# A hybrid decoder trunk on one core: the parts of the attention are moved to later items of the program

## The chip, the cores and the metric

The kernel runs on one NeuronCore of a Trainium2 chip. The metric is the device time of one execution in microseconds, the median of the runs shown. PE is the matmul engine, PEld its weight loads, ACT the scalar engine, DVE the vector engine, POOL the general one, SP the engine whose queue issues most DMAs. PSUM is the memory that PE writes, SBUF the working memory.

## The reference

Two layers on 512 tokens of width 1024, all in float32. Cut to what matters:

```python
h = rmsnorm(x, g_mix[l])
dq, dk, dv, c_q, c_kv_kr, xq, gate_logits = jnp.split(h @ w_in[l], split_idx, axis=-1)
y_diff = diff_attention(dq, dk, dv, ...) @ w_diff_o[l]       # 8 heads, 2 causal softmaxes each: (p0 - lam * p1) v
y_mla = latent_attention(c_q, c_kv_kr, ...) @ w_mla_o[l]     # 8 causal heads, q and k of 96
y_mem = memory_cross_attention(xq, mem_n, ...) @ w_cross_o[l]  # 4 heads into 256 memory tokens
gates = jax.nn.sigmoid((gate_logits + b_gate[l]).reshape(B, S, N_BRANCHES, D))
merged = gates[:, :, 0] * y_diff + gates[:, :, 1] * y_mla + gates[:, :, 2] * y_mem
x = x + merged @ w_out[l]
x = x + jnp.square(jax.nn.relu(rmsnorm(x, g_mlp[l]) @ w_mlp1[l])) @ w_mlp2[l]
```

Queries, keys and several latents are normalised by their root mean square, and queries and keys are rotated by position.

## The kernel before

Weights stream from HBM in units of 128 x 1024 numbers. Each unit is split into a high part `whi` (written by ACT, L101) and a low part `wlo` (DVE, L102), and a product is three matmuls of the parts (`mm3`, L109 to L111). Three raw units and four split ones are held.

A layer is a list of entries, each a function that issues its instructions and the weight units that it needs. `phases` lists the attention entries ("items" here): four head pairs of latent attention (`mla_att`), four cross heads, eight heads of differential attention (`diff_att`), each head with four items, one for each block of 128 queries (cross: two). `PLAN` lists the projections (entries of matmuls with weights) that belong to each phase, and `merge` puts them between the items, about one or two behind each. The projections are: K0, K1, Q0, Q1 (`kvb_item`, `qb_item`) for the latent attention, `mem_chunk`, `xq_chunk`, `head_chunk` (queries and keys of one differential head), `v_chunk`, `gate_item`, and `y4_item`, the output products of the cross and latent attention. Behind the last phase stand `y8_item` (output product of the differential attention), `out_item`, and the MLP.

An item of differential attention does all its parts in one entry: `scores` (matmuls L622, mask L634, maximum L636, exponential L639, the two maps joined at L644), then `pv_tok`: one PE transpose for each block of 128 keys (L650), a copy to SBUF (tile PT, L95), and the value products (L654) into the bank `pso`. After the fourth item, `o_copy` and `o_finish` normalise the head's output and transpose it (L681). Latent and cross attention use L625 for scores, `turned` (transposes L666, copies to the two PT tiles of a split) and `mm3` into `pso`. Projections that need rows turned into columns transpose at the end of their entry: `heads_T` (L482) for keys and queries of the latent attention, L360 and L395 for memory keys and cross queries, L597 for differential heads, the last behind a chain of DVE work that ends at L593.

Pools with few buffers matter: PSUM has two banks `psacc` (projections), three `pss` (scores), two `pstp` (transposes) and one `pso` (values). In SBUF there are three probability tiles `P`, four `PT` and five `scr`.

The order on each engine is made at build time. The library's planner takes the program's instructions with their dependences, runs a timing model of the engines, and at each moment gives an engine the earliest one in the program that the model holds ready; each engine then executes its list strictly in that order, waiting where the real time differs.

Of the kernel before, what the change touches and what calls it, by code (L numbers as in the profile page):

```python
# [59 lines left out]
def tile_trunk(ctx: ExitStack, tc: tile.TileContext, x_t, mem_t, mem_n, pos, ifr, gcol, grow, w_ck, w_cq, w_kvb, w_qb,  # L60
# [36 lines left out]
    def scale_to(o, i, col):  # L97
        A.activation(out=o, in_=i, func=AF.Copy, scale=col)
# [182 lines left out]
    def layer(l):  # L281
        col = lambda c, n=P: gc[:n, l, c:c + 1]
        s = {}

        def build_rope():
# [55 lines left out]
        def mem_chunk(c):  # L341
            def done(tp, q):
                if c < 2:
# [12 lines left out]
                    V.tensor_tensor(out=yv, in0=yv, in1=f[:, :4].unsqueeze(2).broadcast_to([P, 4, 128]), op=ALU.mult)  # L356
                    tp_ = ps("tp")
                    for h in range(2):
                        for t in range(2):
                            T.transpose(tp_[:, h * 256 + t * P:h * 256 + (t + 1) * P], in_=yv[:, t * 2 + h, :], identity=ident)  # L360
                    o = tl("B")
                    scale_to(o, tp_, col(C_CK))
                    s["mk"].append(o)
                else:
# [10 lines left out]
        def xq_chunk(c):  # L375
            def done(tp, q):
# [14 lines left out]
                V.tensor_tensor(out=yv, in0=yv, in1=f[:, :4].unsqueeze(2).broadcast_to([P, 4, 128]), op=ALU.mult)  # L391
                tp_ = ps("tp")
                for h in range(2):
                    for t in range(2):
                        T.transpose(tp_[:, h * 256 + t * P:h * 256 + (t + 1) * P], in_=yv[:, t * 2 + h, :], identity=ident)  # L395
                for h in range(2):
                    scale_to(s["xq", c][h][:, tp * 256:(tp + 1) * 256], tp_[:, h * 256:(h + 1) * 256], col(C_CQ))
            return chunk256(w_xq[l, c], x_h, 4, done)
# [88 lines left out]
        def kvb_item(hf):  # L487
            def fn(w):
# [31 lines left out]
                s["kT", hf], s["v", hf] = [], vv  # L520
                heads_T(kc, s["kT", hf], col(C_MK, 96))
            return Entry(fn, [w_kvb[l, hf]])

        def qb_item(hf):
            def fn(w):
# [26 lines left out]
                s["qT", hf] = []  # L552
                heads_T(qt, s["qT", hf], col(C_MQ, 96))
            return Entry(fn, [w_qb[l, hf][:, 0:2, :], w_qb[l, hf][:, 2:3, :]])
# [10 lines left out]
        def head_chunk(h):  # L565
            def done(tp, q):
# [26 lines left out]
                V.tensor_tensor(out=yg, in0=yg, in1=f.unsqueeze(2).broadcast_to([P, 8, 64]), op=ALU.mult)  # L593
                tp_ = ps("tp")
                for c in range(2):
                    for t in range(2):
                        T.transpose(tp_[:, c * 256 + t * P:c * 256 + (t + 1) * P], in_=y[:, t * 256 + c * P:t * 256 + (c + 1) * P], identity=ident)  # L597
                sl = slice(tp * 256, (tp + 1) * 256)
                for m in range(2):
                    own, oth = slice(m * 64, (m + 1) * 64), slice((1 - m) * 64, (2 - m) * 64)  # L600
                    qs, ks = tp_[own, 0:256], tp_[own, 256:512]
                    copy_to(qh[m][own, sl], qs)
                    copy_to(kk[m][own, sl], ks)
                    copy_to(qh[m][oth, sl], qs)
                    V.tensor_tensor(out=ql[m][own, sl], in0=qs, in1=qh[m][own, sl], op=ALU.subtract)
                    V.tensor_tensor(out=kk[m][oth, sl], in0=ks, in1=kk[m][own, sl], op=ALU.subtract)
            return chunk256(w_d[l, h], x_h, 4, done)
# [38 lines left out]

        def pv_tok(pt, nb, o, vs):
            tp_ = ps("tp")
            for j in range(nb):
                T.transpose(tp_[:, j * P:(j + 1) * P], in_=pt[:, 0, j * P:(j + 1) * P], identity=ident)  # L650
            w = tl("PT")
            copy_to(w[:, :nb * P], tp_[:, :nb * P])
            for j in range(nb):
                T.matmul(o, lhsT=w[:, j * P:(j + 1) * P], rhs=vs(j), start=j == 0, stop=j == nb - 1)  # L654

# [20 lines left out]
        def o_finish(o, f, ng, gain, key):  # L676
            ov = o.rearrange("p (g d) -> p g d", g=ng)
            V.tensor_tensor(out=ov, in0=ov, in1=f.unsqueeze(2).broadcast_to([P, ng, 512 // ng]), op=ALU.mult)
            tp_ = ps("tp")
            for t in range(NT):  # L680
                T.transpose(tp_[:, t * P:(t + 1) * P], in_=o[:, t * P:(t + 1) * P], identity=ident)  # L681
            hi, lo = tl("O", F32R), tl("O", F32R)
            split_scaled(hi, lo, tp_, gain)
            s.setdefault(key, []).append((hi, lo))

        def o_copy():
            c = tl("scr")
            A.activation(out=c, in_=s["co"], func=AF.Copy)
            return c

        def cross_att(h):
            c, hh = h // 2, h % 2

            def unit(qp):
                def fn(w):
                    if qp == 0:
                        s["co"] = ps("o")
# [4 lines left out]
                    w = turned([pt[:, m, j * P:(j + 1) * P] for j in range(2) for m in range(2)])  # L702
                    for j in range(2):
                        mm3(s["co"][:, qp * 256:(qp + 1) * 256], tuple(z[:, j * 256 + hh * P:j * 256 + (hh + 1) * P] for z in s["mv"][c]), tuple(z[:, j * 256:(j + 1) * 256] for z in w), j == 0, j == 1)
                    if qp == 1:
                        o_split("oc")
                return Entry(fn)
            return [unit(0), unit(1)]

        def mla_att(hp):  # L710
            hf, h0 = hp // 2, (hp % 2) * 2

            def unit(qi):
                def fn(w):
# [8 lines left out]
                    pair = (s["pe"], pt)  # L723
                    o = ps("o")
                    ov = o.rearrange("p (m q t) -> p m q t", m=2, q=2)
                    for j in range(qi + 1):
                        g = 1 if j == qi else 0
                        w = turned([x[:, m, j * P:(j + 1) * P] for m in range(2) for x in pair[g:]])
                        f = (j % 2) * 256 + h0 * 64
                        mm3(ov[:, :, 1, :] if g else o, tuple(z[:, f:f + P] for z in s["v", hf][j // 2]),  # L730
                            tuple(z[:, :256] if g else z for z in w), j == 0, j == qi, skip_group_check=True)
                    if qi == 1:
                        s["oT"] = tl("O", F32R), tl("O", F32R)
                    hi, lo = s["oT"]
                    sl = slice((qi - 1) * P, (qi + 1) * P)
                    for m in range(2):
                        r = slice(m * 64, (m + 1) * 64)
                        split_into(hi[r, sl], lo[r, sl], o[r, m * 256:(m + 1) * 256])
                    if qi == NT - 1:
                        s.setdefault("om", []).append((hi, lo))  # L740
                return Entry(fn)
            return [unit(q) for q in range(NT)]

        def diff_att(h):
            p, hh = h // 2, h % 2

            def unit(qi):
                def fn(w):
                    if qi == 0:
                        s["co"], s["cs"] = ps("o"), small("osum", 8, 3)  # L750
                    N = P * (qi + 1)
                    o, cs = s["co"], s["cs"].rearrange("p (m q) -> p m q", m=2)
                    qh, ql, kk = s["dh", h]
# [4 lines left out]
                    pt = scores(N, qk, True, [cs[:, m, qi:qi + 1] for m in range(2)], True)  # L758
                    pv_tok(pt, qi + 1, o[:, qi * P:(qi + 1) * P], vf)
                    if qi == NT - 1:  # L760
                        oc = o_copy()
                        z = tl("scr")
# [7 lines left out]
                        rsq(f[:, :4], e[:, :4], 4)  # L770
                        o_finish(oc, f[:, :4], 4, dgain[:, l:l + 1], "od")
                return Entry(fn)
            return [unit(q) for q in range(NT)]
# [251 lines left out]
```

## Time and profile before

| | us |
|---|---|
| median of 3 runs (lowest to highest) | 2017.84 (2017.49 to 2018.43) |
| the profiled execution's own time | 2019.04 |
| its span, first to last instruction | 2017.2 |
| PE busy | 1976.3 (98%) |
| DVE busy | 1187.2 (59%) |
| ACT busy | 961.9 (48%) |

Times in the rows are from the start of the span. Layer 0 ends near 1017 us, and layer 1 repeats it. Matmuls are pipelined, so the busy time of one is longer than the distance between two.

### The profile page before, as it was taken

What the parts mean: (1) busy time and instruction counts of PE and PEld (TensorE: products, weight loads), DVE (VectorE), ACT (ScalarE), POOL (GpSimd) and SP (SyncE); (2) the same over time, 40 slices, a digit from 0 to 9 for tenths busy, and PEclk for the clock granted to TensorE, in tenths of its full rate; (3) what the DMA queues carried; (4) which work ended last, traced back from release to release, by engine and by line L of the source; (5) the groups of instructions that cost most, each with busy time, mean ns of one, the idle gap of its engine ahead of it and who ended that gap; (6) DMA issues with size and microseconds to landing.
All of it is one profiled execution on the core that took longest, in us unless ns stands there. A gap on an engine that the chain in (4) does not pass through costs nothing.

```text
span 2017.2 us, 27896 instructions
## 1 busy us (share of the span) xinstructions
PE 1976.3 (98%) x10880; PEld 1711.2 (85%) x10880; DVE 1187.2 (59%) x2235; ACT 961.9 (48%) x1855; POOL 155.7 (8%) x153
## 2 busy tenths in 40 slices
PE   8999999999999999999999999999999999999999
PEld 7778989888888888888888899988888888888887
DVE  7756677687745443434447667678777554434442
ACT  5766765555533432323347667556555333323321
POOL 0300101111100000000002001011111000000000
PEclk9989999999999999999999999999999999999999
DMA  5233222222224333333332321221222333333332
GB/s 170 73 107 105 64 64 69 69 71 66 74 76 149 92 102 94 94 100 100 114 109 65 124 86 53 72 76 63 63 74 74 115 115 94 95 95 101 97 94 73
DMA packets 54676, 181.06 MB, mean 90 GB/s; under 512 B 6417, under 2 KB 7441, under 8 KB 54545
## 3 DMA queue, kind: packets, MB, share of 16 engines
q1 hardware_dynamic: 51840, 175.66, 28.1%
q10 hardware_dynamic: 2704, 3.62, 0.6%
q8 instruction: 86, 1.41, 0.3%
q14 instruction: 46, 0.37, 0.1%
HBM read 175.06 MB, written 4.19 MB: 89 GB/s over the span
## 4 chain that ended last, share of the span: by engine, by line
PE 91%; DVE 5%; ACT 2%; issue 1%; DMA 1%; POOL 0%; ACTq 0%; DVEq 0%; POOLq 0%
PE psacc L109 19%; PE psacc L110 19%; PE psacc L111 19%; PE pss L111 7%; PE pss L109 7%; PE pss L110 7%; PE pss L625 2%; PE pso L654 2%; PE pss L622 2%; PE pstp L666 1%; PE pstp L650 1%; DVE wlo L102 1%; PE pso L110 1%; PE pso L111 1%; PE pso L109 1%
## 5 line engine op out<-in xcount | busy, mean ns | idle before, releaser
L101 ACT ACTIVATE whi<-wraw 128x1024 fp32r<-128x1024 f32 (+3 forms) x320 | 334.4, 1046 | 694.3 <-PE psacc L110 353.8
L102 DVE TENSOR_TENSOR wlo<-wraw,whi 128x1024 fp32r<-128x1024 f32 (+3 forms) x320 | 386.0, 1206 | 94.1 <-ACT whi L101 92.0
L109 PE MATMUL psacc<-H,whi 128*128 128x512 f32 x816 | 321.0, 393 | 3.7 <-DVE G L781 3.2
L110 PE MATMUL psacc<-H,whi 128*128 128x512 f32 x816 | 319.1, 391 | 0.0
L111 PE MATMUL psacc<-H,wlo 128*128 128x512 f32 x816 | 319.0, 391 | 0.0
L109 PE MATMUL psacc<-whi,H 128*128 128x256 f32 (+1 forms) x928 | 270.3, 292 | 11.9 <-ACT whi L101 6.9
L110 PE MATMUL psacc<-wlo,H 128*128 128x256 f32 (+1 forms) x928 | 266.4, 287 | 0.9 <-DVE wlo L102 0.9
L111 PE MATMUL psacc<-whi,H 128*128 128x256 f32 (+1 forms) x928 | 265.5, 288 | 0.0
L110 PE MATMUL pss<-O,whi 128*128 128x512 f32 x640 | 249.2, 389 | 0.0
L111 PE MATMUL pss<-O,wlo 128*128 128x512 f32 x640 | 249.2, 390 | 0.0
L109 PE MATMUL pss<-O,whi 128*128 128x512 f32 x640 | 248.9, 390 | 0.0
L109 PEld LDWEIGHTS psacc<-whi,H 128*128 128x128 f32 x928 | 177.8, 192 | 17.0 <-ACT whi L101 6.9
L109 PEld LDWEIGHTS psacc<-H,whi 128*128 128x128 f32 x816 | 153.3, 188 | 35.7 <-DVE G L781 4.1
L110 PEld LDWEIGHTS psacc<-wlo,H 128*128 128x128 f32 x928 | 178.0, 192 | 3.4 <-DVE wlo L102 1.2
L111 PEld LDWEIGHTS psacc<-H,wlo 128*128 128x128 f32 x816 | 153.3, 188 | 31.8
L110 PEld LDWEIGHTS psacc<-H,whi 128*128 128x128 f32 x816 | 153.3, 188 | 29.9
L111 PEld LDWEIGHTS psacc<-whi,H 128*128 128x128 f32 x928 | 177.2, 192 | 0.3
L853 DVE TENSOR_TENSOR X<-psacc,X 128x512 f32<-128x512 f32 x64 | 44.3, 692 | 207.1 <-PE psacc L111 207.1
L109 PEld LDWEIGHTS pss<-O,whi 128*128 128x128 f32 x640 | 120.2, 188 | 25.7 <-DVE B L792 0.6
L110 PEld LDWEIGHTS pss<-O,whi 128*128 128x128 f32 x640 | 120.2, 188 | 24.9
L639 ACT ACTIVATE P<-pss,nmx 128x128 f32<-128x128 f32 (+2 forms) x224 | 115.5, 521 | 53.9 <-DVE nmx L636 34.7
L111 PEld LDWEIGHTS pss<-O,wlo 128*128 128x128 f32 x640 | 120.2, 188 | 24.7
(233 smaller groups left out, 3291.3 us busy)
## 6 DMA issues: line engine op xcount, KB each, us to landing
wraw<-in_w_dram SPq DMA_DIRECT2D x128, 512.0 KB, 3.6
wraw<-in_w_g_dram SPq DMA_DIRECT2D x48, 512.0 KB, 3.6
wraw<-in_w_d_dram SPq DMA_DIRECT2D x48, 512.0 KB, 3.6
wraw<-in_w_mem_dram SPq DMA_DIRECT2D x16, 512.0 KB, 3.6
wraw<-in_w_od_dram SPq DMA_DIRECT2D x16, 512.0 KB, 3.6
wraw<-in_w_out_dram SPq DMA_DIRECT2D x16, 512.0 KB, 3.8
X<-in_x_t_dram SPq DMA_DIRECT2D x16, 256.0 KB, 4.9
wraw<-in_w_xq_dram SPq DMA_DIRECT2D x8, 512.0 KB, 4.6
```

The costliest lines, as they stand in the source:

```text
L101: A.activation(out=hi, in_=src, func=AF.Copy)
L102: V.tensor_tensor(out=lo, in0=src, in1=hi, op=ALU.subtract)
L109: T.matmul(o, lhsT=l[0], rhs=r[0], start=first, stop=False, **kw)
L110: T.matmul(o, lhsT=l[0], rhs=r[1], start=False, stop=False, **kw)
L111: T.matmul(o, lhsT=l[1], rhs=r[0], start=False, stop=last, **kw)
L622: T.matmul(sw[m][:, :max(N, 256)], lhsT=qk[m][0][i], rhs=qk[m][1], start=i == 0, stop=i == 1)
L625: T.matmul(sv[m], lhsT=qk[m][0], rhs=qk[m][1], start=True, stop=True)
L639: A.activation(out=pt[:, m, :N], in_=sv[m], func=AF.Exp, bias=nmx[:, m:m + 1], accum_out=ssum[m])
L650: T.transpose(tp_[:, j * P:(j + 1) * P], in_=pt[:, 0, j * P:(j + 1) * P], identity=ident)
L654: T.matmul(o, lhsT=w[:, j * P:(j + 1) * P], rhs=vs(j), start=j == 0, stop=j == nb - 1)
L666: T.transpose(tp_[:, i * P:(i + 1) * P], in_=b, identity=ident)
L853: V.tensor_tensor(out=xt, in0=q, in1=xt, op=ALU.add)
```

## The change

The attention's parts are put into later entries. Each layer gets a list `pend` and a counter `slot`. `later(n, order, fn)` puts `fn` down for n items later, and `tick()`, called at the start of each item (of each projection in a phase without items), issues what is due, lower `order` first.

- Differential attention: transposes two items behind their scores, value products one item later; the head's end (copy, norm) follows its last value product, and its transposes (L681) one item after that.
- Latent attention: behind the second and fourth item of a pair, transposes of the first two key blocks one item late, those of the last two (fourth item only) two items late, value products one item behind their transposes.
- Cross attention: transposes one item late, products one later.
- Projections (`mem_chunk` keys, `xq_chunk`, `kvb_item`, `qb_item`, `head_chunk`): transposes and what reads them one item late.
- Four ticks in an entry of their own ahead of the first `y8_item` issue what is left. `o_copy` is written out in place, and `pso` is taken when the first value product is issued.

```diff
+        pend, slot = [], [0]
+        def later(n, order, fn):
+            pend.append((slot[0] + n, order, fn))
+        def tick():
+            slot[0] += 1
+            due = sorted((x for x in pend if x[0] <= slot[0]), key=lambda x: x[1])
+            pend[:] = [x for x in pend if x[0] > slot[0]]
+            for x in due:
+                x[2]()
...
-                heads_T(kc, s["kT", hf], col(C_MK, 96))
+                later(1, 0, lambda: heads_T(kc, s["kT", hf], col(C_MK, 96)))
...
+                def turn():
+                    tp_ = ps("tp")
+                    for c in range(2):
+                        for t in range(2):
+                            T.transpose(tp_[:, c * 256 + t * P:c * 256 + (t + 1) * P], in_=y[:, t * 256 + c * P:t * 256 + (c + 1) * P], identity=ident)
...
+                later(1, 0, turn)
...
-        def pv_tok(pt, nb, o, vs):
...
+        def pv_tok(pt, nb, o_of, vs, end):
+            def turn():
+                tp_ = ps("tp")
+                for j in range(nb):
+                    T.transpose(tp_[:, j * P:(j + 1) * P], in_=pt[:, 0, j * P:(j + 1) * P], identity=ident)
+                w = tl("PT")
+                copy_to(w[:, :nb * P], tp_[:, :nb * P])
+
+                def value():
+                    o = o_of()
+                    for j in range(nb):
+                        T.matmul(o, lhsT=w[:, j * P:(j + 1) * P], rhs=vs(j), start=j == 0, stop=j == nb - 1)
+                    end()
+                later(1, 1, value)
+            later(2, 0, turn)
...
+                    def turn(js):
+                        def go():
+                            for j in js:
+                                z[j] = turned([x[:, m, j * P:(j + 1) * P] for m in range(2) for x in pair[j == qi:]])
+                            later(1, 2, lambda: value(js))
+                        return go
...
+                    later(1, 0, turn((0, 1)))
                     if qi == NT - 1:
-                        s.setdefault("om", []).append((hi, lo))
+                        later(2, 3, turn((2, 3)))
...
         for a, sp in zip(phases, PLAN):
-            e += merge(a, take(sp))
+            g = take(sp)
+            for x in a or g:
+                ticking(x)
+            e += merge(a, g)
         assert not any(groups.values())
-        e += [y8_item(ft) for ft in range(KT)]
+        e += [Entry(lambda w: [tick() for _ in range(4)] and None)] + [y8_item(ft) for ft in range(KT)]
```

## Rows read from the trace of the kernel before

**Rows 1.** The page, busy time of each engine, its share and instructions.

```profile
PE 1976.3 (98%) x10880; PEld 1711.2 (85%) x10880; DVE 1187.2 (59%) x2235; ACT 961.9 (48%) x1855; POOL 155.7 (8%) x153
```

**Rows 2.** Busy time of each engine by stretch; the last three: clock, DMA share, GB/s.

```profile
80.00:125.00 45.00, 43.65 (x220) 35.95 (x219) 29.18 (x70) 28.00 (x57) 7.59 (x6) 1.00 0.28 85
125.00:180.00 55.00, 48.60 (x306) 42.50 (x305) 34.57 (x69) 39.15 (x88) 2.71 (x3) 0.91 0.41 129
180.00:305.00 125.00, 125.00 (x881) 115.62 (x880) 83.33 (x167) 82.14 (x196) 15.04 (x14) 1.00 0.19 60
305.00:525.00 220.00, 211.78 (x1454) 194.26 (x1453) 165.13 (x388) 121.28 (x278) 31.64 (x27) 1.00 0.23 70
...
585.00:1000.00 415.00, 415.00 (x1841) 343.58 (x1840) 191.94 (x228) 137.77 (x175) 2.02 (x2) 1.00 0.34 103
...
1084.00:1130.00 46.00, 44.65 (x224) 36.85 (x222) 29.17 (x70) 27.95 (x57) 7.59 (x6) 1.00 0.29 90
1130.00:1175.00 45.00, 43.52 (x312) 39.05 (x312) 32.20 (x62) 35.87 (x80) 2.87 (x2) 1.00 0.39 126
1175.00:1300.00 125.00, 125.00 (x874) 114.91 (x873) 84.38 (x170) 83.65 (x199) 14.40 (x14) 1.00 0.19 60
1300.00:1520.00 220.00, 211.84 (x1446) 194.63 (x1445) 164.41 (x384) 120.07 (x275) 30.91 (x27) 0.99 0.23 70
```

**Rows 3.** PE's waits from 305 to 525: us in total, times, longest.

```profile
PE psacc L109 <- DVE G L792: 1.7, 2, 1.1
PE psacc L109 <- DVE G L781: 1.6, 2, 1.1
PE psacc L109 <- ACT B L562: 1.4, 1, 1.4
PE pstp L597 <- DVE scr L593: 1.4, 2, 1.1
PE pso L654 <- ACT PT L95: 0.5, 1, 0.5
```

**Rows 4.** PE's waits from 80 to 305, two of them.

```profile
PE psacc L109 <- ACT O L105: 2.5, 1, 2.5
PE pso L109 <- ACT PT L101: 1.9, 1, 1.9
```

**Rows 5.** Five of nine idle places in 305 to 525, and all nine's sum.

```profile
368.00:374.00 6.00, 5.20 (x34) 3.99 (x33) 5.48 (x17) 4.23 (x12) 0.00 (x0) 1.00 0.00 0
...
384.00:390.00 6.00, 4.63 (x38) 4.28 (x37) 5.02 (x12) 3.70 (x12) 1.45 (x3) 1.00 0.02 7
409.00:422.00 13.00, 11.35 (x58) 9.11 (x57) 12.52 (x27) 7.12 (x16) 2.85 (x4) 1.00 0.24 82
454.00:462.00 8.00, 6.43 (x52) 6.05 (x52) 5.66 (x14) 4.46 (x12) 2.42 (x3) 1.00 0.04 15
...
483.00:494.00 11.00, 9.00 (x41) 7.00 (x40) 10.85 (x24) 4.61 (x12) 3.13 (x3) 1.00 0.17 51
...
sum 67.00, PE 58.78 PEld 49.52 DVE 58.94 ACT 41.05 POOL 10.00; mean PE 6.53 PEld 5.50 DVE 6.55 ACT 4.56 POOL 1.11
```

**Rows 6.** Groups of instructions from 305 to 525.

```profile
L654 PE MATMUL pso<-B,PT 128*128 128x128 f32 x120 | 17.5, 276 | 0.6 <-ACT PT L95 0.5
...
L650 PE MATMUL pstp<-ident,P 128*128 128x128 f32 x60 | 10.6, 272 | 0.0
```

**Rows 7.** The chain that ended last, pieces from 337 to 349: start, us, what.

```profile
340.65 0.45 PE pstp L597 x4
...
342.84 1.16 PE pso L654 x8
344.00 0.23 PE psacc L109
```

**Rows 8.** Timeline of ACT near 129 us: start, us, instruction, idle before it.

```profile
128.91 0.63 ACT L208 ACTIVATE B<-B 128x512 f32<-128x512 f32 x1 [3.16 <-DMA B<-in_mem_n_dram]
...
129.54 0.58 ACT L101 ACTIVATE PT<-pstp 128x512 fp32r<-128x512 f32 x1
```

More of the change, by code (lines that the diff above doesn't have):

```diff
@@ L391, in done @@
                 V.tensor_tensor(out=yv, in0=yv, in1=f[:, :4].unsqueeze(2).broadcast_to([P, 4, 128]), op=ALU.mult)
[L392 to L397, printed above, removed]
+                def turn():
+                    tp_ = ps("tp")
+                    for h in range(2):
+                        for t in range(2):
+                            T.transpose(tp_[:, h * 256 + t * P:h * 256 + (t + 1) * P], in_=yv[:, t * 2 + h, :], identity=ident)
+                    for h in range(2):
+                        scale_to(s["xq", c][h][:, tp * 256:(tp + 1) * 256], tp_[:, h * 256:(h + 1) * 256], col(C_CQ))
+                later(1, 0, turn)
             return chunk256(w_xq[l, c], x_h, 4, done)
@@ L593, in done, with turn @@
                 V.tensor_tensor(out=yg, in0=yg, in1=f.unsqueeze(2).broadcast_to([P, 8, 64]), op=ALU.mult)
[L594 to L606, printed above, removed]
+                def turn():
+                    tp_ = ps("tp")
+                    for c in range(2):
+                        for t in range(2):
+                            T.transpose(tp_[:, c * 256 + t * P:c * 256 + (t + 1) * P], in_=y[:, t * 256 + c * P:t * 256 + (c + 1) * P], identity=ident)
+                    sl = slice(tp * 256, (tp + 1) * 256)
+                    for m in range(2):
+                        own, oth = slice(m * 64, (m + 1) * 64), slice((1 - m) * 64, (2 - m) * 64)
+                        qs, ks = tp_[own, 0:256], tp_[own, 256:512]
+                        copy_to(qh[m][own, sl], qs)
+                        copy_to(kk[m][own, sl], ks)
+                        copy_to(qh[m][oth, sl], qs)
+                        V.tensor_tensor(out=ql[m][own, sl], in0=qs, in1=qh[m][own, sl], op=ALU.subtract)
+                        V.tensor_tensor(out=kk[m][oth, sl], in0=ks, in1=kk[m][own, sl], op=ALU.subtract)
+                later(1, 0, turn)
             return chunk256(w_d[l, h], x_h, 4, done)
@@ L645, in scores, with turn @@
             return pt
-        def pv_tok(pt, nb, o, vs):
[L648 to L654, printed above, removed]
+        def pv_tok(pt, nb, o_of, vs, end):
+            def turn():
+                tp_ = ps("tp")
+                for j in range(nb):
[9 more added lines that the diff above has]
+            later(2, 0, turn)
         def scaled(pt, N, ssum):
@@ L678, in o_finish, with turn @@
             V.tensor_tensor(out=ov, in0=ov, in1=f.unsqueeze(2).broadcast_to([P, ng, 512 // ng]), op=ALU.mult)
[L679 to L689, printed above, removed]
+            def turn():
+                tp_ = ps("tp")
+                for t in range(NT):
+                    T.transpose(tp_[:, t * P:(t + 1) * P], in_=o[:, t * P:(t + 1) * P], identity=ident)
+                hi, lo = tl("O", F32R), tl("O", F32R)
+                split_scaled(hi, lo, tp_, gain)
+                s.setdefault(key, []).append((hi, lo))
+            later(1, 0, turn)
         def cross_att(h):
@@ L701, in fn, with turn, value @@
                     scaled(pt, 256, cs)
[L702 to L706, printed above, removed]
+                    def turn():
+                        w = turned([pt[:, m, j * P:(j + 1) * P] for j in range(2) for m in range(2)])
+                        def value():
+                            if qp == 0:
+                                s["co"] = ps("o")
+                            for j in range(2):
+                                mm3(s["co"][:, qp * 256:(qp + 1) * 256], tuple(z[:, j * 256 + hh * P:j * 256 + (hh + 1) * P] for z in s["mv"][c]),
+                                    tuple(z[:, j * 256:(j + 1) * 256] for z in w), j == 0, j == 1)
+                            if qp == 1:
+                                o_split("oc")
+                        later(1, 2, value)
+                    later(1, 0, turn)
                 return Entry(fn)
@@ L723, in fn @@
                     pair = (s["pe"], pt)
[L724 to L738, printed above, removed]
+                    z = {}
+                    def turn(js):
[4 more added lines that the diff above has]
+                        return go
@@ new lines, in value @@
+                    def value(js):
+                        if js[0] == 0:
+                            z["o"] = ps("o")
+                        o = z["o"]
+                        ov = o.rearrange("p (m q t) -> p m q t", m=2, q=2)
+                        for j in js:
+                            f = (j % 2) * 256 + h0 * 64
+                            mm3(ov[:, :, 1, :] if j == qi else o, tuple(x[:, f:f + P] for x in s["v", hf][j // 2]),
+                                tuple(x[:, :256] if j == qi else x for x in z[j]), j == 0, j == qi, skip_group_check=True)
+                        if js[-1] < qi:
+                            return
+                        if qi == 1:
+                            s["oT"] = tl("O", F32R), tl("O", F32R)
+                        hi, lo = s["oT"]
+                        sl = slice((qi - 1) * P, (qi + 1) * P)
+                        for m in range(2):
+                            r = slice(m * 64, (m + 1) * 64)
+                            split_into(hi[r, sl], lo[r, sl], o[r, m * 256:(m + 1) * 256])
+                        if qi == NT - 1:
+                            s.setdefault("om", []).append((hi, lo))
@@ L771, in fn @@
                         o_finish(oc, f[:, :4], 4, dgain[:, l:l + 1], "od")
+                    pv_tok(pt, qi + 1, o_of, vf, end)
                 return Entry(fn)
```

40 lines of the change are left out of this document (25 added, 15 removed).

## The prediction

> **What bounds the kernel now.** I read the page first. TensorE (PE) is busy 98% of the span [rows 1], so all idle time that the change could give back is 2017.2 - 1976.3 = 40.9 us. Next the busy time by stretch, to see where it lies [rows 2]. The reader is to subtract PE's busy time from each length. The long MLP stretch has 0.00 us idle in 415. The two middle attention stretches, 180 to 305 and its copy in layer 1, have 0.00 in 125. Idle are: 8.22 and 8.16 us in the two stretches of differential attention (305 to 525, 1300 to 1520), 1.35 twice where the latent attention's scores begin (80, 1084), and 6.40 and 1.48 just after (125, 1130). Those six make 26.96 us; the rest of the 40.9 lies at the start and the end, where nothing is moved. One more loss stands in the same rows: the granted clock between 125 and 180 is 0.91 of full, that is part of the time at 1.2 instead of 2.4 GHz after idle spells, worth at most 0.09 x 55 = 4.95 us.
>
> A rule of the Trainium skill weighs against reading it so: "Perfetto Trace Analysis", section "Identifying the Most-Contended Engine", holds matmul busy time to be a poor measure of what is left and wants the busy share of weight loads, which here is 85% [rows 1]; by that the room would be some 300 us. The trace disagrees: the MLP stretch loads weights for 83% of its time (343.58 of 415.00) and yet has no gap, 1841 matmuls at 225 ns [rows 2]. So 83% is a full engine here.
>
> Then the waits inside 305 to 525 [rows 3]: the five shown make 6.6 us. The three largest wait for an accumulator bank to be drained (DVE L792 1.7, DVE L781 1.6, ACT L562 1.4): the pool psacc has two banks. Two, 1.4 us, are the transposes of a head's projection that come before DVE has finished L593; one, 0.5, is a value product waiting for the copy of its transposes. The stretches around the nine idle places [rows 5] show why: in the 67 us that they cover DVE is busy 58.94 and PE 58.78. In 409 to 422 DVE works 12.52 of 13 us. DVE is not full over the whole stage (165.13 of 220 [rows 2]), it is full in bursts, and PE stands when its next instruction needs that burst's end.
>
> **The change part by part.** No instruction is added or removed: the same transposes, copies and products are issued, only their place in the program moves. The order on the engines is not the program's: a planner lays the instructions out at build time, and program order is its priority among those that it holds ready. So what a move does is to change which ready work PE takes first.
>
> *Transposes two items late, value products three.* The work that becomes freely placeable: 60 transposes and 120 records of value products in 305 to 525 [rows 6], 0.45/4 = 0.11 us and 1.16/8 = 0.145 us each [rows 7], so 6.75 + 17.4 = 24.2 us over 24 items, 1.0 us an item. Today each follows its softmax closely and is taken as soon as it is ready, ahead of projection matmuls; afterwards projection matmuls of two items go ahead of it and it is left over for the moments when those stand still. Lower end: nothing, if the planner does not see the idle places coming (they come where real durations differ from its own). Upper end, with 1.0 us of such work at each of the nine places: their idle times are 0.80, 1.37, 1.65, 1.57 and 2.00 us in the five shown and 8.22 - 7.39 = 0.83 in the other four together, so 0.80 + 4 x 1.0 + 0.83 = 5.63 us a layer. I take two thirds, 3.75, because the stretch 180 to 305, where PE has projections, transposes and products to choose from, shows what enough ready work does: no idle at all [rows 2]. Two layers: 7.5 us.
>
> *Value products' own wait.* The 0.5 us of L654 on ACT's copy [rows 3] goes, since product and copy are now an item apart: 1.0 us in two layers.
>
> *Projections' transposes one item late.* For the eight head projections the transposes of the second token half were already emitted last before the next item; that place hardly moves, so I leave the 1.4 us of L597 in. Only the first half's go behind the 24 matmuls of the second. Nothing taken; bounds 0 and 2 x 1.4 = 2.8 us gained. For the latent, cross and memory projections the next item begins where they stood: nothing.
>
> *Latent attention.* The 1.9 us that a value product waits for the copy PT [rows 4] comes from ACT being held: it waits 3.16 us for a DMA of mem_n and reaches the copy only at 129.54 [rows 8]. ACT works in the order laid out, so a later product finds the same queue. The 2.5 us on ACT L105 [rows 4] are the memory tokens themselves, on the same queue. I take 1.0 of the 10.6 us idle in the four latent stretches, and 1.0 of the 4.95 us of clock; bounds 0 and all.
>
> *What is late next.* Emission puts the last latent value product just ahead of the first y4 item (ym), whose fourth operand it makes. Nine matmuls at 0.23 us [rows 7] cover 2.1 us of a copy chain whose nearest row is 1.9 us: nothing taken, up to 1.9 a layer if the cover is gone. At the layer's end the last head's transposes follow two more gate items and, in y8, 21 matmuls that do not need it, 24 x 0.23 + 21 x 0.23 = 10 us: covered. Buffers: a probability tile (three) lives two items longer, but an item of this stage is 220/24 = 9 us and the third tile carries it.
>
> Sum: 7.5 + 1.0 + 1.0 + 1.0 = 10.5 us. The profiled execution took 2019.04 us, so 2008.5; the median shown is 1.2 below it, so 2007.3, say **2007 us**.
>
> **The rivals.** *Nothing moves (2014 to 2021, taken as 2018).* 4.7 of the 6.6 us in [rows 3] wait for an accumulator bank, and the change leaves those at two. The Trainium skill says the same in "Perfetto Trace Analysis", section "Optimization Strategy": gaps that repeat on the engine that should be full can mean that too little SBUF or PSUM is left for the next tile. For it: the planner already reorders (the chain has a value product inside one projection's matmuls [rows 7]). Against it: PE could run something else while a bank drains.
>
> *Slower (2022 to 2034, taken as 2026).* One mechanism: the four PT buffers. A head pair's last unit needs eight of them, so its second set of transposes waits for the first set's products; and the next pair's transposes are emitted ahead of the products that still read the second set. Its copies then stand on ACT and DVE, and behind them stand the weight splits (L101, L102) that feed PE. That is 2 x (4 + 3) = 14 places. At 1.9 us each, the one copy wait that the trace shows [rows 4], they cost 27 us: 2034. It decides from (10.5 + 4) / 14 = 1.04 us a place. Against it: the places lie mostly where PE idles 0.00 us of 125 [rows 2], with projections to cover them.
>
> *All of it (1986 to 2001, taken as 1996).* Both differential stretches close (16.4) and the clock stays up (5): 21 us. With the rest of the idle too: 2017.8 - 27 - 5 = 1986. It needs DVE's bursts to be spread, since the products drawn apart keep scores from running ahead.
>
> **How the numbers follow.** Forecast 0.51 (own range 2002 to 2013), nothing moves 0.19, slower 0.18, all of it 0.12. About 0.2%, 4 us, is what a measurement of this kernel can tell from no change. Faster is then 0.51 + 0.12 = 0.63, same 0.19, slower 0.18. The range runs from 1994, inside the largest gain, to 2026, the middle of the slow case; it leaves out some 0.05 below and 0.09 above, and covers the bounds 0 to 11 of the first term, 2.8 of the projections' and 3.8 of ym's.
>
> **What the profile of the changed kernel would show.** Right: idle PE in the stretches of differential attention falls from 8.2 to about 4 us each; L650 and L654 stand inside the former gaps; the wait of L654 on PT is gone; the waits for L792 and L781 shrink but stay. The MLP stretch stays as it is, and so does the ACT wait for mem_n. Wrong: idle time in 180 to 305, or ACT and DVE copies PT waiting for products (the slow case); or the same nine places with the same releasers (nothing moves). What would make the whole wrong is that the planner lays out the unmoved stages anew as well.

## The result, and the profile after the change

The changed kernel takes 2030.88 us (median of four runs, 2029.57 to 2031.08); the kernel before took 2018.13 beside it (2017.49 to 2019.21). The ratio is 1.0061 with a 95% interval of 1.0044 to 1.0079: **slower by 12.7 us**, where 2007 was forecast. The forecast has the wrong sign, and the time lies outside its range.

The page of the kernel after, busy time of each engine; it answers to [rows 1]:

```profile
PE 1979.1 (98%) x10880; PEld 1711.6 (84%) x10880; DVE 1188.1 (59%) x2235; ACT 959.7 (47%) x1855; POOL 156.6 (8%) x153
```

Its span is 2027.4 us. PE's idle time is 2027.4 - 1979.1 = 48.3 us, 7.4 more than before, and PE's busy time is 2.8 us longer with the same 10880 instructions. The two make the 10.2 us by which the span grew. The busy time by stretch, in the columns of [rows 2], shows where. The windows from 313 on in layer 0 are set 8 us later than before: the stage of differential attention begins only 1.4 us later (its first joined probabilities end at 300.35, before at 298.98), but the MLP stretch behind it begins 8 us later, so most of the 10.2 us is lost in layer 0.

```profile
125.00:180.00 55.00, 49.48 (x323) 42.78 (x322) 35.43 (x71) 38.67 (x88) 2.71 (x3) 0.94 0.40 129
180.00:250.00 70.00, 70.00 (x533) 65.90 (x532) 42.70 (x90) 48.69 (x112) 10.28 (x10) 1.00 0.20 61
250.00:313.00 63.00, 59.26 (x369) 52.85 (x368) 40.13 (x78) 35.15 (x89) 5.48 (x4) 0.97 0.18 58
313.00:533.00 220.00, 209.89 (x1420) 191.84 (x1419) 164.29 (x382) 118.63 (x272) 30.55 (x26) 0.99 0.22 68
...
593.00:1008.00 415.00, 415.00 (x1841) 343.52 (x1840) 190.71 (x226) 137.36 (x174) 1.01 (x1) 1.00 0.33 103
...
1138.00:1183.00 45.00, 44.71 (x333) 41.56 (x332) 31.49 (x60) 33.84 (x77) 2.01 (x2) 1.00 0.40 127
1183.00:1308.00 125.00, 123.13 (x854) 112.36 (x853) 84.33 (x172) 84.60 (x200) 14.69 (x14) 1.00 0.20 60
1308.00:1530.00 222.00, 211.91 (x1444) 194.26 (x1444) 163.96 (x382) 118.57 (x272) 30.89 (x26) 0.99 0.22 70
```

The early latent stretches got a little better, as forecast: 5.52 us idle instead of 6.40, and 0.29 instead of 1.48. The stretch that was gapless before now has 3.74 us idle in layer 0 (250 to 313) and 1.87 in layer 1 (1183 to 1308). The stages of differential attention, which the change was expected to fill, have 10.11 and 10.09 us idle in these windows where they had 8.22 and 8.16. The MLP stretch is as it was.

What PE waits for from 313 to 533, the counterpart of [rows 3] (L857 was L792, L587 was L562, L846 was L781, L679 was L650):

```profile
PE psacc L109 <- DVE G L857: 4.6, 3, 2.2
PE psacc L109 <- ACT B L587: 3.1, 4, 1.4
PE psacc L109 <- DVE G L846: 1.0, 1, 1.0
PE pstp L679 <- ACT PT L95: 0.7, 2, 0.4
PE pss L650 <- ACT P L667: 0.3, 2, 0.2
```

The waits for a projection's bank, which the forecast let shrink, grew: 4.6 for the y4 drain instead of 1.7, 3.1 for the value copy instead of 1.4. The other two went away (the value product's copy 0.5, the head's transposes waiting for their DVE chain 1.4). One of these places, DVE's timeline of the kernel after, then PE's:

```profile
417.27 0.69 DVE L664 TENSOR_REDUCE nmx<-pss 128x1 f32<-128x512 f32 x1
417.88 0.68 DVE L829 TENSOR_REDUCE ss<-scr 128x4 f32<-128x512 f32 x1
418.48 0.16 DVE L606 TENSOR_TENSOR e<-ss,ex 128x8 f32<-128x8 f32 x1
418.55 0.76 DVE L613 TENSOR_TENSOR scr<-scr,rb 128x256 f32<-128x256 f32 x2
419.23 0.15 DVE L831 TENSOR_TENSOR e<-osum 128x4 f32<-128x4 f32 x1
419.31 0.67 DVE L857 SCALAR_TENSOR_TENSOR G<-G,psacc 128x512 f32<-128x512 f32 x1
```

```profile
417.39 0.47 PE L650 MATMUL pss<-B,B 128*128 128x256 f32 x2
420.03 0.50 PE L109 MATMUL psacc<-O,whi 128*128 128x512 f32 x1 [2.17 <-DVE G L857]
```

The y4 drain (L857) stands in DVE's list behind a score's maximum, a head's norm (L829, L831) and another head's chain (L606, L613), and PE's next projection needs its bank. And here the loss goes on behind the wait. Busy time of the kernel after in the wait and in the 3 us that follow, in the columns of [rows 2]:

```profile
416.00:420.00 4.00, 1.75 (x8) 1.03 (x6) 3.96 (x11) 1.45 (x4) 1.22 (x1) 1.00 0.40 135
420.00:423.00 3.00, 2.97 (x8) 2.40 (x9) 2.89 (x9) 0.00 (x0) 1.43 (x2) 0.61 0.00 0
```

DVE is busy 3.96 of 4 us while PE stands, and the granted clock of the following 3 us is 0.61, most of it at 1.2 instead of 2.4 GHz. That is not so behind every such wait: another one of 2.17 us for L857 ends at 493.27, and the granted clock from 493 to 497 is 1.00.

In 250 to 313, where PE did not wait before, the longest wait is this one, and ACT's timeline shows its cause:

```profile
PE psacc L109 <- ACT O L101: 2.6, 1, 2.6
```

```profile
271.84 2.10 ACT L95 ACTIVATE B<-pstp 64x256 fp32r<-64x256 f32 x6
273.97 0.38 ACT L101 ACTIVATE O<-pso 64x256 fp32r<-64x256 f32 x1
```

The first y4 item (ym) needs the last latent value product split into `O`; that split stands behind six copies of a head's transposed queries and keys, and PE starts at 274.40.

### The profile page after: what moved, and what is told of

Its sections match the earlier page's. It is cut to its first block, busy times and chain, and to the rows that moved or that the text cites. A ratio compares the mean times of both kernels' runs of the same rounds, so it can differ in the third digit from the quotient of the medians.

```text
span 2027.4 us, 27892 instructions
## 1 busy us (share of the span) xinstructions
PE 1979.1 (98%) x10880; PEld 1711.6 (84%) x10880; DVE 1188.1 (59%) x2235; ACT 959.7 (47%) x1855; POOL 156.6 (8%) x153
## 3 DMA queue, kind: packets, MB, share of 16 engines
q1 hardware_dynamic: 51840, 175.66, 27.7%
## 4 chain that ended last, share of the span: by engine, by line
PE 92%; DVE 4%; ACT 3%; DMA 1%; issue 0%; POOL 0%; ACTq 0%
PE psacc L109 20%; PE psacc L110 20%; PE psacc L111 19%; PE pss L111 7%; PE pss L110 7%; PE pss L109 7%; PE pss L653 2%; PE pss L650 1%; PE pso L686 1%; PE pstp L701 1%; PE pstp L679 1%; PE pso L109 1%; PE pso L110 1%; PE pso L111 1%; PE pstp L507 1%; ACT whi L101 1%
## 5 line engine op out<-in xcount | busy, mean ns | idle before, releaser
L109 PE MATMUL psacc<-whi,H 128*128 128x256 f32 (+1 forms) x928 | 267.9, 289 | 13.5 <-ACT whi L101 6.8
L134 POOL TENSOR_TENSOR f<-e,mhalf 128x8 f32<-128x8 f32 (+1 forms) x60 | 89.2, 1487 | 683.0 <-DVE e L606 492.7
```

What stands on the lines that cost most here:

```text
L109: T.matmul(o, lhsT=l[0], rhs=r[0], start=first, stop=False, **kw)
L134: G.tensor_tensor(out=o, in0=e, in1=mhalf[:, :n], op=ALU.pow)
```

## The experiments

All runs stand against the kernel before, whose median beside them is 2019 to 2020 us. The first question was which part of the change costs the 12.7 us. These theories go through the quoted texts. Theory 1: the late transposes of the head projections cost, in its first form because their copies on ACT wait for DVE's subtractions; 1a, because the attention's transposes go ahead of them (with it, that the two `pstp` banks are too few); 1b, because a head's two halves come together; 1c, the planner's layout is merely sensitive. Theory 2: the late attention itself costs. Theory 3: the latent attention's late end makes ym wait. Theory P: three probability tiles P, when they are held long, are a useful brake, which keeps the next scores' work out of the head's chain on DVE.

**Parts undone.** In `head_chunk`, `pv_tok` and `mla_att` in turn:

```diff
# e1: head projections' transposes at once
-                later(1, 0, turn)
+                turn()
# e2: differential attention at once
-                later(1, 1, value)
-            later(2, 0, turn)
+                value()
+            turn()
# e3: latent attention at once
-                            later(1, 2, lambda: value(js))
+                            value(js)
...
-                    later(1, 0, turn((0, 1)))
+                    turn((0, 1)[:qi + 1])()
-                        later(2, 3, turn((2, 3)))
+                        turn((2, 3))()
# e4: e2 + e3 + cross attention at once; only projections' transposes late.  e7: e1 + e3
```

> The changed kernel with one part undone: a differential head's projection transposes at the end of its own entry again, everything else stays late. Theory 1 (the head's two halves are now turned together, and their 12 copies on ACT and 8 subtractions on DVE stand in front of the drains of the accumulator banks, L587 and L857, and in front of the latent products' splits): the waits for those two releasers fall from 9.2 and 6.2 us to about the 3.4 and 2.9 of before, and the time from 2031 to 2018 to 2023. Theory 2 (the late transposes and products of the attention are what costs): less than 3 us change, 2028 to 2032. Theory 3 (the latent products end too late for the first y4 item): the idle 3.7 us around 250 to 313 stays, 2028 to 2032.

> The changed kernel with the differential attention's transposes and products at once behind their scores, as before; projections, latent and cross attention stay late. Theory 1 (head copies): the stretches of differential attention stay at about 10 us idle each, 2028 to 2034. Theory 2 (late products cost): idle there falls to 8.2 us or below, 2024 to 2027. The predicted mechanism (late products fill gaps): idle there rises above 10 us, 2034 or more.

> The changed kernel with the latent attention's transposes and products at once, as before; the rest stays late. Theory 3 (the last latent product reaches the first y4 item too late): idle around 250 to 313 falls from 3.7 us to nearly 0 and in layer 1 from 1.9 to 0, but some 2 us come back where the latent scores begin (125 to 180 and its copy); together 2024 to 2028. Theory 1: at most 1 us, 2029 to 2032.

> Differential, latent and cross attention all at once behind their scores as before; only the projections' transposes stay an item late. Theory 1 (head copies are the cost): 2024 to 2031, clearly above before. Theory 2 or 3 (late attention is the cost): 2016 to 2021, as before.

> Heads' projections and the latent attention at once, differential and cross attention late. If the cost of the late latent products (theory 3) is separate, it adds to the gain of the heads at once: the idle 2.0 us around 250 to 313 and 2.0 in layer 1 go, 2 to 3 us come back where the latent scores begin: 2009 to 2014. If it only arose together with the heads' late copies, it gives 2013 to 2017.

| late parts | us | ratio to before (95%) |
|---|---|---|
| all (the change) | 2030.9 | 1.0061 (1.0044 to 1.0079) |
| all but head transposes (e1) | 2013.9 | 0.9973 (0.9963 to 0.9982) |
| all but differential attention (e2) | 2024.6 | 1.0026 (1.0017 to 1.0035) |
| all but latent attention (e3) | 2025.8 | 1.0031 (1.0020 to 1.0042) |
| projections' transposes only (e4) | 2018.9 | 1.0000 (0.9991 to 1.0008) |
| differential and cross attention, other projections (e7) | 2012.3 | 0.9963 (0.9951 to 0.9976) |

One line of the change, the head transposes' `later`, costs 17.0 us, but only beside late attention: with all attention at once (e4) the late projections cost nothing. Nor is late differential attention dear by itself: in the changed kernel it costs 6.3 us (e2), but with heads and latent attention at once (e7) it stands in a kernel that is some 7 us faster than before. Late latent attention costs 5.0 us in the changed kernel; the 1.5 us between e1 and e7 are within the intervals. In e1 the sign of the forecast is restored. Its stretches, 250 to 313, 313 to 593 and 1308 to 1588, with the page's row:

```profile
PE 1969.9 (98%) x10880; PEld 1706.5 (85%) x10880; DVE 1193.2 (59%) x2235; ACT 960.8 (48%) x1855; POOL 153.8 (8%) x153
```

```profile
250.00:313.00 63.00, 60.97 (x396) 55.07 (x395) 42.31 (x85) 38.22 (x95) 4.47 (x4) 1.00 0.20 59
313.00:593.00 280.00, 273.63 (x1739) 245.49 (x1738) 206.74 (x467) 149.85 (x334) 40.89 (x38) 1.00 0.23 70
...
1308.00:1588.00 280.00, 273.31 (x1728) 244.81 (x1728) 207.53 (x467) 152.03 (x336) 34.50 (x30) 1.00 0.22 69
```

The whole stages of differential attention in the kernel before (first two) and after (last two):

```profile
305.00:585.00 280.00, 271.78 (x1758) 245.11 (x1757) 203.94 (x468) 152.13 (x341) 39.73 (x37) 1.00 0.24 72
1300.00:1580.00 280.00, 271.84 (x1750) 245.54 (x1749) 203.78 (x467) 150.77 (x339) 34.38 (x29) 0.99 0.24 72
```

```profile
313.00:593.00 280.00, 269.37 (x1723) 241.93 (x1722) 205.54 (x468) 149.96 (x337) 41.33 (x38) 0.99 0.23 71
1308.00:1588.00 280.00, 269.91 (x1740) 243.25 (x1740) 204.85 (x468) 151.24 (x341) 34.62 (x29) 0.99 0.23 70
```

6.37 and 6.69 us idle in 280, against 8.22 and 8.16 before and 10.63 and 10.09 after. Of the 16.9 us between the spans of e1 (2010.5) and of the changed kernel, 7.7 are idle time (40.6 against 48.3) and 9.2 are time that PE is busy with the same matmuls. The mean granted clock of the whole run goes with that: 0.999 in e1, 0.996 after, which over 2010 us is 6 us. The profiled e1 is one of its faster runs; by the medians over all runs, 0.998 and 0.9955, it is 5 us.

**Order or lag?** The head transposes one item late, but in the tick ahead of the attention's (e5); the changed kernel with attention's transposes three items behind (e13, with two more ticks at the end); the heads at once with attention only one item behind (e14); only a head's second token half late (e6).

```diff
# e5
-                later(1, 0, turn)
+                later(1, -1, turn)
# e13 (pv_tok)
-            later(2, 0, turn)
+            later(3, 0, turn)
# e14: e1, and in pv_tok
-            later(2, 0, turn)
+            later(1, 0, turn)
# e6
-                later(1, 0, turn)
+                later(1, 0, turn) if tp else turn()
```

> The changed kernel with the head projections' transposes still an item late, but first in their tick, ahead of the attention's transposes (order -1 in place of 0). Theory 1a (what hurts is that the attention's transposes of the item before are put ahead of the heads' transposes, in the two transpose banks and on ACT and DVE): about 2014, as with the heads at once. Theory 1b (what hurts is that the first half is held back until the second half's matmuls are issued, so that both halves come together): it stays near 2030. Theory 1c (the planner's layout is merely sensitive, no part of the order is to blame by itself): anything between.

> The changed kernel with the first half of a head projection turned at once and only the second half an item late, behind the attention's transposes. Theory 1a: near 2030, or halfway for one half of two (2022). Theory 1b: about 2014 to 2016.

> The changed kernel with one number changed: the differential transposes three items behind their scores in place of two; the heads' transposes stay late and behind those of the attention. Theory P (while a head projection's chain runs on DVE, scores that find a free probability tile put their mask, maximum and join into the same stretch of DVE, and the drains of the accumulator banks wait behind both; transposes that come later hold the three tiles longer and keep the scores out): the scores are held again, as with the heads at once, and it goes to 2010 to 2018. Theory 1a (transposes of the attention ahead of the heads' transposes are bad in themselves): the order in the tick is the same, so 2027 to 2034.

> The heads' transposes at once (the variant of 2014), and the differential transposes one item behind their scores in place of two. Theory P: a probability tile is free an item sooner, scores run into the head's chain, and the gain goes: 2017 to 2028. Theory 1a: the heads' transposes still stand ahead of the attention's, so 2012 to 2016.

Measured: e5 2013.9 (0.9973, 0.9964 to 0.9982), e13 2015.1 (0.9972, 0.9960 to 0.9983), e14 2034.0 (1.0067, 1.0054 to 1.0079), e6 2007.6 (0.9941, 0.9929 to 0.9954).

Two of these were to tell theory 1a from theory P, and neither theory came out whole. In e13 the attention's transposes still go first in the tick, so 1a expected 2027 to 2034; P expected 2010 to 2018, rightly. For e14 1a expected 2012 to 2016 and P 2017 to 2028, and it came out slower than both. One order fits all five kernels, but it was read off after they had run, and no later run tests it. Among the kernels with late differential attention, take the head projection behind an item and ask which the program issues first, its transposes or the attention's transposes of the item one before. The attention's stand first in the changed kernel (2030.9) and in e14 (2034.0), the head's in e1 (2013.9), e5 (2013.9) and e13 (2015.1). Within each group the attention's lag and the heads' lateness differ by an item; the time goes by this order. For the changed kernel itself e5 shows it, with a single number changed. e5 also refutes 1b: both halves still come together, and nothing is lost. e6 has one half on either side and is better than either, and than 1a or 1b expected, so a plain "head first" isn't the whole rule. In e14 PE waits for the same drains, over the whole run:

```profile
PE psacc L109 <- DVE G L846: 10.4, 4, 3.3
PE psacc L109 <- DVE G L857: 7.8, 6, 1.7
```

**What makes that order dear?** Three candidates. Banks: `pss` 2 and `pstp` 3 in the changed kernel (e8) and in e1 (e11). Probability tiles: a fourth P, for which two of the 24 tiles B had to go, so each with a control that has 22 B and three P. Copies: in `turn()` all six head copies ahead of the four subtractions (e19).

```diff
# e8: the change, e11: e1, with (PSUM pools, parts of a line)
-("s", 3), ("tp", 2)
+("s", 2), ("tp", 3)
...
# e18: the change, e17: e1, with (parts of a line)
-("B", 24)
+("B", 22)
# e16: e18, e15: e17, with
-    p_p = pool("P", 3)
+    p_p = pool("P", 4)
# e19
                         copy_to(qh[m][oth, sl], qs)
+                    for m in range(2):
+                        own, oth = slice(m * 64, (m + 1) * 64), slice((1 - m) * 64, (2 - m) * 64)
+                        qs, ks = tp_[own, 0:256], tp_[own, 256:512]
                         V.tensor_tensor(out=ql[m][own, sl], in0=qs, in1=qh[m][own, sl], op=ALU.subtract)
...
```

> The changed kernel with three banks for transposes and two for scores, in place of two and three. Theory 1a in the form that the two transpose banks are the scarce thing: the waits for L857 and L587 fall to the 5 us each of the kernel with the heads at once, and the time to 2015 to 2022. If banks are not it: 2028 or more, since the scores lose one.

> Control for the run with three transpose banks and two score banks (2035, against 2031 with two and three): the same exchange in the variant with the heads at once (2014). If banks for transposes are what the late heads lacked, the exchange costs here what the lost score bank costs, 15 us or more (2030), and there it gave that back. If they are not, it costs about the same 4 us: 2016 to 2020.

> The changed kernel with 22 B tiles and four probability tiles. Theory P: scores run into the chain already, so within 4 us of its control, or slower. The rival: within 4 us as well; a gain of 6 us or more would say that the late heads lack tiles, against both.

> Control: the changed kernel (heads late, 2031) with 22 B tiles in place of 24. 2028 to 2036.

> The control with 22 B tiles and the heads at once, and four probability tiles in place of three. Theory P (the tiles hold the scores out of the heads' chain on DVE): with a fourth tile scores get in, and it loses 6 us or more against its control. The rival (the order of the banks by itself): no loss, within 3 us or faster.

> Control: the heads' transposes at once (the variant of 2014), with 22 B tiles in place of 24. No theory says much of it; 2012 to 2022.

> The changed kernel with the six copies of a turned head half issued ahead of its four subtractions, in place of three, two, three, two. Theory 1 in its first form (copies on ACT that wait for DVE stand in front of the drains of the accumulator banks): ACT's 17.5 us of waiting for L633 go, PE's waits for L587 and L857 fall towards 3 us each, and the time to 2012 to 2020. If that wait is not the cost: 2027 to 2034.

| | attention's transposes first (the change) | head's first (e1) | distance |
|---|---|---|---|
| as it is | 2030.9 | 2013.9 | 17.0 |
| pss 2, pstp 3 (e8, e11) | 2035.0, 1.0078 (1.0064 to 1.0092) | 2026.2, 1.0028 (1.0016 to 1.0039) | 8.8 |
| 22 B (e18, e17) | 2042.2, 1.0124 (1.0108 to 1.0139) | 2027.5, 1.0044 (1.0030 to 1.0058) | 14.6 |
| 22 B, four P (e16, e15) | 2028.6, 1.0051 (1.0039 to 1.0064) | 2022.5, 1.0022 (1.0012 to 1.0032) | 6.1 |
| copies first (e19) | 2028.1, 1.0037 (1.0025 to 1.0050) | | |

The exchange of banks costs 4.1 us in one order and 12.3 in the other, between the 4 and the 15 that e11's text names. It takes a score bank away while it gives a transpose bank, so whether more transpose banks alone would help stays open. A fourth P tile gains 13.5 and 5.0 us in kernels with 22 B, so three are a shortage there and no useful brake, against theory P; it takes 8.5 of the 14.6 us of distance away, and 6.1 stay. Two tiles B fewer, which no theory was about, cost 11.3 and 13.7 us, as much as the whole effect under study and more than either control's text expected.

A part of each distance lies in the clock. The median granted clock of the runs, attention's transposes first against head's first, is 0.9955 against 0.998 as it is, 0.992 against 0.995 with the banks exchanged, 0.991 against 0.996 with 22 B and 0.992 against 0.9945 with four P as well; times the run that is some 5, 6, 10 and 5 us, an estimate. So of the 6.1 us that stay with four P most go with the clock. No run sets the clock apart from the waits ahead of it.

In e19 ACT no longer waits for the subtractions (17.5 us in the changed kernel, all places together, and none here), yet the time falls by only 2.8 us (4.8 by the ratios to before, whose intervals overlap). And ACT's wait was nothing new: in the kernel before (L606 was L633) and in e1 it is as long. The three in this order, before, after, e1:

```profile
ACT B L95 <- DVE B L606: 18.5, 20, 2.1
```

```profile
ACT B L95 <- DVE B L633: 17.5, 14, 2.5
```

```profile
ACT B L95 <- DVE B L633: 17.2, 14, 3.3
```

PE's waits of e19 over the whole run (L849 is the changed kernel's L846), and its stages of differential attention:

```profile
PE psacc L109 <- DVE G L849: 10.8, 4, 2.7
...
PE psacc L109 <- ACT B L587: 4.5, 8, 0.8
```

```profile
313.00:593.00 280.00, 272.03 (x1737) 245.52 (x1736) 205.55 (x470) 150.98 (x339) 40.67 (x38) 0.99 0.24 71
...
1308.00:1588.00 280.00, 272.05 (x1755) 246.15 (x1754) 204.69 (x468) 152.34 (x340) 36.90 (x30) 0.99 0.24 71
```

So the copies' wait does not set the changed kernel apart from before or from e1; taken away, it leaves another drain late. The stages idle 7.97 and 7.95 us here, no more than before, while the time is 8 us above it: the median granted clock of e19's runs is 0.993, against 0.996 in the runs of before beside them, some 6 us of 2028. Idle time alone doesn't rank these kernels.

**The best version.** e12 is e6 with the latent attention at once (e3's edit); e20 is e12 with the copies first (e19's edit).

> The fastest so far (first half of a head turned at once, second half late: 2008) with the latent attention at once as well. If the late latent products cost their idle 2.7 us around 250 to 313 and its copy apart from the rest: 2003 to 2007. If what they give where the latent scores begin makes up for it: 2007 to 2010.

> The fastest variant so far (first half of a head at once, second late, latent attention at once: 2003), with the copies first as well. Its ACT does not wait for L633, so theory 1 expects 2000 to 2006; a gain or loss of more than 4 us would say that the order of the copies works in another way, too.

Measured: 2003.2 (0.9913, 0.9899 to 0.9926) and **1999.6 (0.9897, 0.9882 to 0.9912)**, the fastest of all, 20 us below before and 31 below the change. The page's row of e20, its stretches 250 to 313, 313 to 593 and 1308 to 1588, and two of PE's waits over the whole run:

```profile
PE 1973.6 (99%) x10880; PEld 1711.6 (86%) x10880; DVE 1190.5 (59%) x2235; ACT 959.9 (48%) x1855; POOL 153.3 (8%) x153
```

```profile
250.00:313.00 63.00, 63.00 (x421) 57.82 (x419) 40.79 (x80) 38.67 (x95) 4.48 (x4) 1.00 0.22 67
313.00:593.00 280.00, 278.93 (x1773) 250.94 (x1772) 211.13 (x476) 153.30 (x343) 39.40 (x38) 1.00 0.23 70
1308.00:1588.00 280.00, 278.93 (x1743) 249.44 (x1743) 212.46 (x474) 152.53 (x337) 34.24 (x30) 1.00 0.25 76
```

```profile
PE psacc L109 <- ACT B L587: 0.9, 4, 0.2
...
PE pss L656 <- ACT P L670: 0.8, 2, 0.6
```

Idle in each stage of differential attention is 1.07 us, in the whole span of 2001.3 us 27.7, and no wait for a y4 or gate drain is left in the list of PE's waits.

## Why the prediction was wrong

**The step that failed is "Projections' transposes one item late".** It took nothing, with bounds of 0 and 2.8 us gained, since "that place hardly moves". It looked at where the transposes stand against their own projection; what counted was where they stand against the attention's transposes, which the same change moves. Undoing that one line gives 17.0 us back, changing only its order in the tick (e5) the same, and without late attention (e4) it costs 0. What it costs shows as PE's waits for a projection's bank, whose drains stand behind other work, and as a lower clock. The step had no lower bound for a loss, and the parts were summed as if they were independent.

**"What is late next" was the second.** It named the right place (the last latent value product just ahead of ym) and priced the copy chain at 1.9 us, but took nothing because nine matmuls cover 2.1. The trace has 2.6 us of wait there: the nearest row was a chain whose ACT a DMA had held [rows 8], and here six head copies (2.10 us) stand ahead of it. Latent attention at once gives 5.0 us (e3) or 4.4 (e12 against e6) back; the 1.5 between e7 and e1 are not clear of noise.

**Filling the gaps, 7.5 us.** Idle time in the two stages of differential attention falls from 8.22 and 8.16 us to 6.37 and 6.69 in e1 and to 1.07 in each in e20. In e1 that is 3.3 us of the 7.5, and it is not what makes e1 faster than before: idle time of its whole run is 40.6 us against 40.9, since the latent stretches lost what these gained (2.03 us idle from 250 to 313, where before had none). PE is busy 6.4 us less in e1; the granted clock of the two profiled runs, 0.999 against 0.996, makes some 6 us of that, the medians over all runs, 0.998 against 0.997, only 2. So the forecast's mechanism is borne out in e1 for the stage and not for the time. In e20 the gaps do close, 13 us less idle in the whole run; that the late products are what fills them was not tested, since no run has e20's other edits with the differential attention at once.

The picture of before was wrong, too. The forecast says that "each follows its softmax closely". Counted from the ends of L644 to the starts of L650 item by item (mean over both layers' stages), the transposes stood 13.9 us behind their joined probabilities in before, and the scores of 2.2 later items had begun by then; the planner had already drawn them apart. In the changed kernel (L672 and L679) it is 15.9 us and 2.5 items. Two items in the program became 0.3 on the engine. That this made the gain small is likely, but no run shows it.

**The value products' wait, 1.0 us,** was right: no L686 (before L654) stands among the waits of 313 to 533. **Latent and clock, 1.0 each:** the early latent stretches gained 0.88 and 1.19 us of idle time; the new idle of 3.74 and 1.87 us behind them took more. The granted clock of 125 to 180 is 0.94 instead of 0.91 in the two profiled runs, which one run of each can't put down to the change; the median of the whole run fell to 0.9955, from 0.997 in the runs of before beside e1 to e4.

**The rivals.** The slower case ended on the right side, and its sign, idle time in 180 to 305, came, but by another mechanism than the one told. A shortage of PT hardly shows: ACT waits 5.6 us for products that still read those tiles, 4.2 before, and all of PE's waits for copies and splits into PT make 2.9 us in the whole run, 2.8 before. The y4 stretch lost through ACT's queue. "Nothing moves" had the right places (bank drains stay the largest waits), but they grew. The rule it named from the Trainium skill ("Perfetto Trace Analysis", "Optimization Strategy", gaps from too little SBUF or PSUM) bore out in part: a fourth P tile gains 5.0 and 13.5 us where two B are missing; for the accumulator banks, which the forecast named, no run shows it. But e20 closes the gaps without any more buffers. "All of it", 1996, needed e6's split and two more edits: e20 is at 1999.6.

**What stays open** is why the planner's lists come out so much worse when the attention's transposes stand first. Shown are that the order of the head transposes in the tick decides in the changed kernel (e5), and the place of the loss (PE at psacc, DVE and ACT drains standing behind a burst of other heads' work). The copies' wait and the two halves alone are excluded, the P tiles are part of it where two B are missing, the clock takes a part, and the banks could not be separated, since the runs gave one pool a bank by taking it from another.

## What to carry to other kernels

When a planner lays out the order and program order is its priority, a move is a change of priority: price each moved step against every other step that moves, not against its old neighbours, and let the sum of the parts have a bound for their interaction. Before counting on a pipeline to create slack, measure in the trace how far apart the planner has put the stages already. Then undo the parts one at a time: here one reordered line turned +12.7 us into -5, and splitting it by halves into -12.

## What the runs showed that was not expected

Two of the 24 tiles B fewer cost 11.3 and 13.7 us (e18, e17), so a study that buys a buffer by taking another away needs a control of its own. And the price of a stall can be more than its length: behind one 2.17 us wait the granted clock was 0.61 for 3 us, behind another there was no such loss, and 9.2 of the 16.9 us between the spans of e1 and the changed kernel lie in time that PE is busy, not in idle time.
